# A fourth pair of split-weight tiles in place of one load buffer, and the fold products spread over four pieces

## The chip, the core and the metric

The kernel runs on one core of a Trainium2 chip. The metric is the device time of one execution in microseconds. A TensorE matmul is called PE here, its weight load PEld, VectorE is DVE, ScalarE is ACT, and SP is the queue that issues the loads.

## The reference, cut to what matters

Two layers of a decoder run over 256 tokens of width 1024. The change touches only the last part of the second layer, a mixture of eight experts:

```python
def moe_swiglu(t, router, w_gate, w_up, w_down):
    logits = (t @ router).astype(jnp.float32)
    top_logits, top_idx = lax.top_k(logits, TOP_K)          # TOP_K = 2 of 8
    gates = jax.nn.softmax(top_logits, axis=-1)
    combine = ...                                           # (tokens, experts)
    for e in range(N_EXPERTS):
        out = out + combine[:, e:e + 1] * swiglu(t, w_gate[e], w_up[e], w_down[e])

def swiglu(t, w_gate, w_up, w_down):
    return (jax.nn.silu(t @ w_gate) * (t @ w_up)) @ w_down  # 1024 -> 3584 -> 1024
```

All weights and activations are float32. The products keep nearly float32 precision: each float32 operand is split into a high part (a cast to fp32r) and a low part (what the cast left), and high by high, low by high and high by low are summed.

## The kernel before, in words

The experts are worked on one after the other, in the order of how many tokens they got, and alternate between two kinds (`KIND = "LSLSLSLS"`). A large one has room for 128 tokens. A small one has room for 64; the high and low parts of its 64 tokens lie side by side as the 128 columns of one stationary operand.

An expert's weights come in *pieces* of 128x1024 floats (512 KB), 84 for an expert. One load brings a unit of two pieces. `load` (L1182) takes its buffer from `ring`, a list of pools that is used round and round. At this stage the list holds 17 units: three of pool `wraw` (two 512 KB transfers each), two of `a8p`, one of `wraw3` (`NRAW3`), four of `wraw0` and seven of `wraw2`. SP issues a load as soon as its buffer is free, and a buffer is free when DVE has read its second piece.

`split_raw` (L181) makes a piece's pair of tiles out of pool `whl`, which holds three pairs: `split_to` (L188) lets ACT cast the piece to `whi` (L189), then DVE subtracts to get `wlo` (L190). A pair may be written again when PE has read it: the high tile after PE's products with it (L1497), the low tile after the products with the low part (L1499).

The order of the instructions on PE, ACT and DVE is that of the program (`in_order`); no engine overtakes within its own list. `piece` (L1488) first calls `run_ahead` (L1479), which writes down splits until `1 + AHEAD` pieces are split and not yet used, and then hands out the oldest. So with `AHEAD = 2` the split of piece n+2 stands in the lists before PE's products of piece n, and all that follows piece n in the program stands behind that split on ACT and DVE.

A group of twelve pieces is `gate_up` of one block of 512 hidden columns (L1501, four pieces for the gate, four for up; they are called g1 to g8 below) and `down` of the block before (L1568, four pieces, d1 to d4). A large expert's piece takes six products of 512 columns, a small one's four.

Small steps are laid between the pieces. `after(n, f)` (L1364) runs f behind the n-th piece from then on, as counted by `tick`. For a small expert `fold` (L1532) turns the two sums of a block and adds their halves:

- `turned` (L1538): eight products of 64 columns with the constant `fold` into one PSUM tile `hT`, all after the fourth piece (PE shows each float32 product as two instructions);
- `silu` on ACT (L1546) and `times` on DVE (L1551) after the eighth, `parts` after the eleventh, which splits the result into `mhh` (ACT, then DVE). `mhh` is the stationary operand of the next `down`.

The sums that `turned` reads are copied out of PSUM by ACT three pieces after their products (L1521). At the very end of the last expert the counts are 2, 3, 3 and 4.

`dispatch` (L1384) gathers the tokens of the next expert: DVE writes `sel` (L1392, L1394), PE multiplies with it (L1400, L1425), and ACT and DVE split the result into `X`. It is run in steps between the pieces of `down` of the fifth and sixth block. `combine` (L1583) adds an expert's result into `h` in the same way.

Of the kernel before, what the change touches and what calls it, by code (L numbers as in the profile page):

```python
# [11 lines left out]
F32R = mybir.dt.float32r  # L12
# [18 lines left out]
NEG = -1.0e30  # L31
NWRAW = 6
NRAW2 = 7
NRAW3 = 1
NRAW0 = 4
AHEAD = 2
PRE = 2


# [67 lines left out]
def build(tc, I, out, dbg=None, upto=99):  # L107
    with ExitStack() as es:
        _build(tc, tc.nc, es, I, out, dbg or {}, upto)


def _build(tc, nc, es, I, out, dbg, upto):
    const = es.enter_context(tc.tile_pool(name="const", bufs=1))
    wraw = es.enter_context(tc.tile_pool(name="wraw", bufs=NWRAW))
    whl = es.enter_context(tc.tile_pool(name="whl", bufs=3))
    small = es.enter_context(tc.tile_pool(name="small", bufs=2))

    def left(stack, name, bufs):
        return stack.enter_context(tc.tile_pool(name=name, bufs=bufs, reuse_waits="tile"))

    def right(stack, name, bufs):
        return stack.enter_context(tc.tile_pool(name=name, bufs=bufs, side="right", reuse_waits="tile"))
# [18 lines left out]
    def ps(shape, name, tag="ps"):  # L141
        return banks[tag].tile(shape, F32, name=name, tag=tag)
# [15 lines left out]
    def dump(name, ap):  # L158
        if name in dbg:
            nc.sync.dma_start(dbg[name], ap)  # L160
# [13 lines left out]
    def stream(src, n, piece=1024):  # L174
        raws = load_pieces(src, n, piece)

        def split(i):
            return split_raw(raws[i])
        return split

    def split_raw(raw):  # L181
        w = raw.shape[-1]
        hi = whl.tile([128, 1024], F32R, name="whi", tag="whi")
        lo = whl.tile([128, 1024], F32R, name="wlo", tag="wlo")
        split_to(hi[:, :w], lo[:, :w], raw)
        return hi[:, :w], lo[:, :w]

    def split_to(hi, lo, src):  # L188
        nc.scalar.copy(out=hi, in_=src)  # L189
        nc.vector.tensor_tensor(out=lo, in0=src, in1=hi.bitcast(F32), op=OP.subtract)  # L190
# [25 lines left out]
    def C(k):  # L216
        for offs, t in ((_COFF, cst), (_LOFF, csl), (_KOFF, csk)):
            if k in offs:
                o, n = offs[k]
                return t[:, o:o + n]  # L220
# [9 lines left out]
    def preload(func, after=None):  # L230

        after = eps if after is None else after.bitcast(F32)
        nc.scalar.activation(dummy, after, func, bias=eps, scale=0.0)
# [330 lines left out]
    with ExitStack() as l0:  # L564
# [272 lines left out]
        def finish(p, table=False):  # L837

            if not ya:
                ya.append(Blocks(4, "ya", b4))  # L840
            Yc = c4(Y[p])
            st = rt.tile([128, 3, 4], F32, name="st")
            nc.vector.tensor_scalar(st[:, 0, :], mv[p][:, :, 1], 64e-5, None, op0=OP.add)
            if table:
                nc.scalar.activation(st[:, 2, :], st[:, 0, :], AF.Sqrt)
            nc.vector.tensor_tensor(out=Yc, in0=Yc, in1=mv[p][:, :, 0:1].to_broadcast([128, 4, 64]), op=OP.subtract)
            if table:
                nc.vector.reciprocal(st[:, 2, :], st[:, 2, :])
            else:
                rsqrt(st[:, 2, :], st[:, 0, :], st[:, 1, :])  # L850
            bd = blockdiag("KR")[:, 0]
            for s in halves:
                nc.vector.tensor_tensor(out=bd[s, :, s], in0=Yc[s],
                                        in1=st[s, 2, :, None].to_broadcast([64, 4, 64]), op=OP.mult)
            yield
            g = ps([128, 4, 128], "yT", f"pp{p % 2}" if table else "ps")
            for c in range(4):
                nc.tensor.transpose(g[:, c, :], bd[:, c, :], ident)
            y_ = b1("yl")
            for s in halves:  # L860
                nc.vector.scalar_tensor_tensor(c4(y_[s]), g[s, :, s], V("lg", p)[s], c4(bonus[p][s]),
                                               op0=OP.mult, op1=OP.add)
            yield
            nc.vector.tensor_tensor(out=y_, in0=y_, in1=gg[p], op=OP.mult)
            hi, lo = ya[0](p)
            split_to(hi, lo, y_)
            yield
# [135 lines left out]
        end = [finish(2, True), finish(3, True)]  # L1003
# [21 lines left out]
    with ExitStack() as l0:  # L1025
# [40 lines left out]
        a8p = right(es, "a8", 2)  # L1066
# [23 lines left out]
    with l1:  # L1090
# [89 lines left out]
        ring = [wraw0] * NRAW0  # L1180

        def load(src, eng=None):  # L1182
            p = ring.pop(0)
            ring.append(p)
            if p is wraw:
                return stream(src, 2048)
            raw = a8([128, 2048], "mraw") if p is a8p else p.tile([128, 2048], F32, name="mraw", tag="mraw")
            (eng or nc.sync).dma_start(raw, src)
            return lambda i: split_raw(raw[:, i * 1024:(i + 1) * 1024])
# [167 lines left out]
    def experts(kinds, late=None, hook=None):  # L1357
# [6 lines left out]
        def after(n, f):  # L1364
            deferred.append([n, f])
# [112 lines left out]

        def run_ahead(n=1 + AHEAD):  # L1479
            while len(ready) < n and (raws or units):  # L1480
                if not raws:
                    load_unit()
                    if not units:
                        gf[0] = gain("final_norm", t=wraw.tile([128, D], F32, name="raw", tag="raw"), eng=nc.sync)
                sp, i = raws.pop(0)
                ready.append(sp(i))
# [14 lines left out]
        def gate_up(e, fc):  # L1501
            large = kinds[e] == "L"
            acc = []
            sums = {}
            for w in range(2):
                a = ps([128, 512], "gu", "gu")
                for i in range(4):
                    wh, wl = piece()
                    terms = []
                    for k in range(2):  # L1510
                        kb = 2 * i + k
                        c = slice(k * 512, (k + 1) * 512)
                        x = (X[e][:, 0, kb, :], X[e][:, 1, kb, :]) if large else X[e][:, kb, :]
                        terms.append((a, x, (wh[:, c], wl[:, c]), kb == 0, kb == 7))
                    products(large, terms)
                    tick()
                    next(side[0], None)
                acc.append(a)
                if not large:
                    t = sums[w] = mt.tile([128, 512], F32, name=("msg", "mhl")[w], **({} if w else {"bufs": 1}))  # L1520
                    after(1 if (e, fc) == (last, NFC - 1) else 3, lambda t=t, a=a: nc.scalar.copy(out=t, in_=a))  # L1521
            end = (e, fc) == (last, NFC - 1)
            if not large:
                return fold(sums, end)
            sgt = mt.tile([128, 512], F32, name="msg", bufs=1)
            nc.scalar.activation(sgt, acc[0], AF.Silu)
            if end:
                preload(AF.Sqrt)
            nc.vector.tensor_tensor(out=sgt, in0=sgt, in1=acc[1], op=OP.mult)
            return sgt  # L1530

        def fold(sums, end):  # L1532

            H = mt.tile([128, 4, 128], F32R, name="mhh")
            t = mt.tile([128, 512], F32, name="mhl").rearrange("p (w f t) -> p w f t", w=2, f=4)
            pt = []

            def turned():  # L1538
                pt.append(ps([128, 2, 4, 64], "hT", "hT"))
                for w in range(2):  # L1540
                    for f in range(4):
                        nc.tensor.matmul(pt[0][:, w, f, :], lhsT=sums[w][:, f * 128:(f + 1) * 128], rhs=C("fold"),
                                         start=True, stop=True)

            def silu():
                nc.scalar.activation(t[:, 0], pt[0][:, 0], AF.Silu)  # L1546
                if end:
                    preload(AF.Sqrt)

            def times():  # L1550
                nc.vector.tensor_tensor(out=t[:, 1], in0=t[:, 0], in1=pt[0][:, 1], op=OP.mult)  # L1551

            def parts():
                split_to(H[:, :, 0:64], H[:, :, 64:128], t[:, 1])
            for n, f in zip((2, 3, 3, 4) if end else (4, 8, 8, 11), (turned, silu, times, parts)):
                after(n, f)
            return H

# [126 lines left out]
    before.close()  # L1685
    mt = left(es, "moet", 2)
    mo = left(es, "moe", 1)
    wraw3 = left(es, "wraw3", NRAW3)
    ring[:0] = [wraw] * (NWRAW // 2) + [a8p] + [wraw3] * NRAW3
    dump("h3", h)  # L1690
    if upto <= 3:
        return
# [108 lines left out]
```

## Time and profile before

| | before |
|---|---|
| runs, median (lowest to highest) | 1545.63 us (1540.59 to 1546.87), 3 runs |
| the profiled execution, its time and its span | 1547.02 us, 1545.2 us |
| PE busy in the span | 1457.0 us (94%) |
| DVE busy | 1248.5 us (81%) |
| ACT busy | 1047.4 us (68%) |
| loads | 426.86 MB in all, mean 276 GB/s |

The page's table of slices shows that the experts fill the span from about 550 us to 1530 us. In that part PE and DVE have nine tenths or more in nearly every slice, and so do the DMA engines. Shares of busy time therefore don't tell what limits this part; it has to be read from single stretches. In the order of time a row gives the start, the length from the first start to the last end, and in brackets the idle time before it and what ended it. Instructions of one engine overlap at their ends, so the pace is read from one start to the next and not from the length. What a queue waits for is a row "who <- whom".

### The profile page before, as it was taken

Reading aid. Unit: us, or ns where it says so; the run is one execution under the profiler, and the core shown is the slowest. Engines: PE = TensorE matmul, PEld = TensorE weight load, DVE = VectorE, ACT = ScalarE, POOL = GpSimd, SP = SyncE. Lnnn points to the kernel's source line nnn. Section 1 sums busy time; section 2 is a strip of 40 time slices with the busy share of each in tenths; the row PEclk is TensorE's granted clock in tenths of the full one; section 3 lists DMA queues with packets and bytes.
Section 4 is the critical chain, followed back from the end, with each engine's and each line's share of the span. In section 5 each row is a group of like instructions: output and inputs, shape, how many; then the busy total and the mean of one; then the engine's idle time right before and its main releaser. Section 6 shows DMA issues by size and latency. Waiting matters only on the chain. (4 is left out here: it accounts for less than half of the span.)

```text
span 1545.2 us, 22471 instructions
## 1 busy us (share of the span) xinstructions
PE 1457.0 (94%) x7781; PEld 1196.7 (77%) x7781; DVE 1248.5 (81%) x1634; ACT 1047.4 (68%) x1440; POOL 85.6 (6%) x154
## 2 busy tenths in 40 slices
PE   7889999999999999999999999999999999999894
PEld 6879888998798887776778886678886667887673
DVE  6786775554586579989989989989989989989995
ACT  6634345444455568778878778878768878768884
POOL 4223120001010010000000000000000000000000
PEclk9999999999999999999999999999999999999997
DMA  8230035558453869989999989999989989999941
GB/s 303 67 108 15 1 97 190 186 183 298 152 191 116 320 235 351 345 329 375 395 364 374 369 329 378 384 371 377 361 337 372 383 360 382 372 352 349 368 181 32
DMA packets 78275, 426.86 MB, mean 276 GB/s; under 512 B 9200, under 2 KB 9472, under 8 KB 42560
## 3 DMA queue, kind: packets, MB, share of 16 engines
q1 hardware_dynamic: 77328, 422.38, 73.3%
q0 software_dynamic: 816, 2.87, 0.6%
q8 instruction: 65, 1.06, 0.3%
q14 instruction: 66, 0.54, 0.1%
HBM read 424.15 MB, written 1.05 MB: 275 GB/s over the span
## 5 line engine op out<-in xcount | busy, mean ns | idle before, releaser
L190 DVE TENSOR_TENSOR wlo<-mraw,whi 128x1024 fp32r<-128x1024 f32 x556 | 659.9, 1223 | 67.5 <-ACT whi L189 51.7
L189 ACT CAST whi<-mraw 128x1024 fp32r<-128x1024 f32 x556 | 570.6, 1050 | 151.3 <-PE gu L1497 79.6
L1497 PE MATMUL gu<-whi,x 128*128 128x512 f32 x1344 | 384.5, 394 | 0.6 <-ACT whi L189 0.5
L190 DVE TENSOR_TENSOR wlo<-raw,whi 128x1024 fp32r<-128x1024 f32 x232 | 280.3, 1222 | 109.2 <-ACT whi L189 104.9
L189 ACT CAST whi<-raw 128x1024 fp32r<-128x1024 f32 x232 | 239.6, 1043 | 135.6 <-PE acc L194 37.9
L1499 PE MATMUL gu<-wlo,x 128*128 128x512 f32 x896 | 291.6, 407 | 10.8 <-DVE wlo L190 10.3
L1497 PEld LDWEIGHTS gu<-whi,x 128*128 128x128 f32 x1344 | 250.2, 188 | 55.4 <-ACT whi L189 1.0
L1499 PEld LDWEIGHTS gu<-wlo,x 128*128 128x128 f32 x896 | 159.1, 188 | 82.4 <-DVE wlo L190 54.6
L1497 PE MATMUL Y<-whi,mhh 128*128 128x512 f32 x448 | 165.7, 411 | 19.9 <-DVE mhh L190 19.9
L1499 PE MATMUL Y<-wlo,mhh 128*128 128x512 f32 x448 | 144.9, 405 | 3.1 <-DVE wlo L190 2.2
L1497 PEld LDWEIGHTS Y<-whi,mhh 128*128 128x128 f32 x448 | 82.1, 190 | 45.4 <-DVE mhh L190 30.8
L1499 PEld LDWEIGHTS Y<-wlo,mhh 128*128 128x128 f32 x448 | 81.6, 190 | 34.2 <-DVE wlo L190 17.6
L193 PE MATMUL cp<-u,whi 128*128 128x256 f32 (+1 forms) x360 | 101.9, 283 | 0.0
L195 PE MATMUL cp<-u,whi 128*128 128x256 f32 (+1 forms) x360 | 101.8, 283 | 0.0
L194 PE MATMUL cp<-u,wlo 128*128 128x256 f32 (+1 forms) x360 | 101.8, 283 | 0.0
L1497 PE MATMUL Y<-whi,mhl 128*128 128x512 f32 x224 | 87.7, 391 | 0.0
L194 PEld LDWEIGHTS cp<-u,wlo 128*128 128x128 f32 (+1 forms) x360 | 68.3, 190 | 0.3
L193 PEld LDWEIGHTS cp<-u,whi 128*128 128x128 f32 (+1 forms) x360 | 68.3, 190 | 0.3
L195 PEld LDWEIGHTS cp<-u,whi 128*128 128x128 f32 (+1 forms) x360 | 68.3, 190 | 0.2
L1497 PEld LDWEIGHTS Y<-whi,mhl 128*128 128x128 f32 x224 | 42.2, 188 | 8.0
L193 PE MATMUL tp<-whi,u 128*128 128x512 f32 x96 | 40.6, 423 | 2.4 <-DVE u L190 2.4
L194 PE MATMUL tp<-whi,u 128*128 128x512 f32 x96 | 39.6, 413 | 2.2 <-DVE u L190 2.2
(425 smaller groups left out, 1967.5 us busy)
## 6 DMA issues: line engine op xcount, KB each, us to landing
mraw<-in_moe SPq DMA_DIRECT2D x277, 1024.0 KB, 7.0
raw<-in_moe SPq DMA_DIRECT2D x116, 512.0 KB, 6.6
raw<-in_ffn_gu SPq DMA_DIRECT2D x44, 512.0 KB, 3.7
raw<-in_w_in SPq DMA_DIRECT2D x38, 512.0 KB, 3.6
raw<-in_ffn_d SPq DMA_DIRECT2D x22, 512.0 KB, 3.5
raw<-in_w_out SPq DMA_DIRECT2D x16, 512.0 KB, 3.6
raw<-in_w_in SPq DMA_DIRECT2D x4, 416.0 KB, 9.0
h<-in_x SPq DMA_DIRECT2D x2, 512.0 KB, 6.1
```

Of the source, the lines that this page charges most:

```text
L189: nc.scalar.copy(out=hi, in_=src)
L190: nc.vector.tensor_tensor(out=lo, in0=src, in1=hi.bitcast(F32), op=OP.subtract)
L193: nc.tensor.matmul(o, lhsT=a[0], rhs=b[0], start=start, stop=False)
L194: nc.tensor.matmul(o, lhsT=a[1], rhs=b[0], start=False, stop=False)
L195: nc.tensor.matmul(o, lhsT=a[0], rhs=b[1], start=False, stop=stop)
L1497: nc.tensor.matmul(o, lhsT=x, rhs=b[0], start=start and i == 0, stop=False)
L1499: nc.tensor.matmul(o, lhsT=a[0] if large else a, rhs=b[1], start=False, stop=stop)
```

## The change

One load buffer is given up (`NRAW3` and pool `wraw3`, one unit of 1 MB), and its room goes to a new pool `whl2` with one pair of split tiles. `split_raw` takes its tiles from the four pairs in turn, and `AHEAD` becomes 3: the split of piece n+3 stands before PE's products of piece n. Before the experts begin there are three pairs as before.

The eight fold products are cut into four parts of two, placed after the second, third, fourth and fifth piece; `silu` goes from the eighth to the seventh, `times` stays at the eighth, and `parts` goes from the eleventh to the tenth. At the end of the last expert the counts stay.

```diff
--- before.py
+++ after.py
@@ -31,9 +31,8 @@
 NEG = -1.0e30
 NWRAW = 6
 NRAW2 = 7
-NRAW3 = 1
 NRAW0 = 4
-AHEAD = 2
+AHEAD = 3
 PRE = 2
 
 
@@ -178,10 +177,14 @@
             return split_raw(raws[i])
         return split
 
+    parts_ = [whl] * 3
+
     def split_raw(raw):
         w = raw.shape[-1]
-        hi = whl.tile([128, 1024], F32R, name="whi", tag="whi")
-        lo = whl.tile([128, 1024], F32R, name="wlo", tag="wlo")
+        p = parts_.pop(0)
+        parts_.append(p)
+        hi = p.tile([128, 1024], F32R, name="whi", tag="whi")
+        lo = p.tile([128, 1024], F32R, name="wlo", tag="wlo")
         split_to(hi[:, :w], lo[:, :w], raw)
         return hi[:, :w], lo[:, :w]
 
@@ -1535,12 +1538,12 @@
             t = mt.tile([128, 512], F32, name="mhl").rearrange("p (w f t) -> p w f t", w=2, f=4)
             pt = []
 
-            def turned():
-                pt.append(ps([128, 2, 4, 64], "hT", "hT"))
-                for w in range(2):
-                    for f in range(4):
-                        nc.tensor.matmul(pt[0][:, w, f, :], lhsT=sums[w][:, f * 128:(f + 1) * 128], rhs=C("fold"),
-                                         start=True, stop=True)
+            def turned(w, fs):
+                if not pt:
+                    pt.append(ps([128, 2, 4, 64], "hT", "hT"))
+                for f in fs:
+                    nc.tensor.matmul(pt[0][:, w, f, :], lhsT=sums[w][:, f * 128:(f + 1) * 128], rhs=C("fold"),
+                                     start=True, stop=True)
 
             def silu():
                 nc.scalar.activation(t[:, 0], pt[0][:, 0], AF.Silu)
@@ -1552,7 +1555,9 @@
 
             def parts():
                 split_to(H[:, :, 0:64], H[:, :, 64:128], t[:, 1])
-            for n, f in zip((2, 3, 3, 4) if end else (4, 8, 8, 11), (turned, silu, times, parts)):
+            for i in range(4):
+                after(2 if end else 2 + i, lambda i=i: turned(i // 2, range(2 * (i % 2), 2 * (i % 2) + 2)))
+            for n, f in zip((3, 3, 4) if end else (7, 8, 10), (silu, times, parts)):
                 after(n, f)
             return H
 
@@ -1685,8 +1690,8 @@
     before.close()
     mt = left(es, "moet", 2)
     mo = left(es, "moe", 1)
-    wraw3 = left(es, "wraw3", NRAW3)
-    ring[:0] = [wraw] * (NWRAW // 2) + [a8p] + [wraw3] * NRAW3
+    ring[:0] = [wraw] * (NWRAW // 2) + [a8p]
+    parts_.append(left(es, "whl2", 1))
     dump("h3", h)
     if upto <= 3:
         return
```

## Rows read from the trace of the kernel before

**Rows 1.** Busy time by stretch: a large expert, then a small one's DVE-paced stretch
```profile
core 0: us, PE busy (x) PEld busy (x) DVE busy (x) ACT busy (x) POOL busy (x), PEclk, DMA share, GB/s
805.00:925.00 120.00, 118.77 (x549) 97.63 (x548) 109.65 (x106) 93.12 (x102) 0.00 (x0) 1.00 0.95 358
925.00:1015.00 90.00, 84.20 (x373) 60.78 (x371) 85.44 (x85) 76.41 (x93) 0.00 (x0) 1.00 0.99 385
```

**Rows 2.** Waits in 925 to 1015 us: us in total, times, longest
```profile
DVE wlo L190 <- ACT whi L189: 4.5, 5, 1.5
PE Y L1497 <- DVE mhh L190: 2.8, 4, 1.1
```

**Rows 3.** The same view, 1406 to 1511 us, the last expert
```profile
DVE wlo L190 <- ACT whi L189: 5.3, 6, 1.5
```

**Rows 4.** DVE in order of time: start, length, what, count, idle before it
```profile
985.14 3.49 DVE L190 TENSOR_TENSOR wlo<-mraw,whi 128x1024 fp32r<-128x1024 f32 x3
988.55 3.49 DVE L190 TENSOR_TENSOR wlo<-raw,whi 128x1024 fp32r<-128x1024 f32 x3
992.79 2.36 DVE L190 TENSOR_TENSOR wlo<-raw,whi 128x1024 fp32r<-128x1024 f32 x2 [0.76 <-ACT whi L189]
```

**Rows 5.** ACT in order of time, same stretch
```profile
991.72 2.95 ACT L189 CAST whi<-raw 128x1024 fp32r<-128x1024 f32 x3 [1.29 <-PE gu L1497]
```

**Rows 6.** PE in order of time, same stretch
```profile
988.17 0.62 PE L1497 MATMUL Y<-whi,mhh 128*128 128x512 f32 x2
989.26 1.00 PE L1542 MATMUL hT<-csk,msg 128*128 128x64 f32 x8
990.10 1.06 PE L1542 MATMUL hT<-csk,mhl 128*128 128x64 f32 x8
990.96 0.71 PE L1497 MATMUL gu<-whi,x 128*128 128x512 f32 x2
991.52 0.63 PE L1499 MATMUL gu<-wlo,x 128*128 128x512 f32 x2
991.98 0.62 PE L1497 MATMUL gu<-whi,x 128*128 128x512 f32 x2
```

**Rows 7.** PE in order of time, a large expert
```profile
872.72 1.08 PE L1497 MATMUL gu<-whi,x 128*128 128x512 f32 x4
874.10 1.08 PE L1497 MATMUL gu<-whi,x 128*128 128x512 f32 x4
```

**Rows 8.** DVE in order of time, after a large expert
```profile
943.56 3.50 DVE L190 TENSOR_TENSOR wlo<-raw,whi 128x1024 fp32r<-128x1024 f32 x3 [1.48 <-ACT whi L189]
```

**Rows 9.** DVE and PE in order of time, dispatch of a large expert
```profile
1017.68 0.48 DVE L1392 TENSOR_SCALAR sel<-iota,route 128x128 f32<-128x128 int16 x2
1020.75 1.23 DVE L190 TENSOR_TENSOR wlo<-mraw,whi 128x1024 fp32r<-128x1024 f32 x1 [1.46 <-ACT whi L189]
...
1018.01 1.16 PE L1400 MATMUL xT<-sel,un 128*128 128x128 f32 x8 [1.28 <-DVE sel L1392]
```

**Rows 10.** Busy time by stretch: twelve pieces at two dispatches, two us within one
```profile
1008.97:1029.28 20.31, 18.03 (x100) 14.13 (x99) 15.05 (x17) 13.79 (x18) 0.00 (x0) 1.00 0.95 383
1248.85:1270.74 21.89, 19.59 (x100) 15.50 (x99) 15.05 (x17) 13.79 (x18) 0.00 (x0) 0.92 0.87 354
...
1258.00:1260.00 2.00, 2.00 (x10) 1.90 (x11) 1.17 (x2) 0.00 (x0) 0.00 (x0) 0.57 1.04 430
```

**Rows 11.** Waits in 805 to 925 us, a large expert
```profile
PE xT L1425 <- DVE sel L1394: 1.1, 1, 1.1
```

**Rows 12.** PE in order of time, first expert
```profile
627.73 0.73 PE L1499 MATMUL Y<-wlo,mhh 128*128 128x512 f32 x2 [0.78 <-DVE wlo L190]
```

**Rows 13.** SP's waits; DMA issues (count, size, us to landing); a late stretch
```profile
SPq L1188 <- DVE wlo L190: 513.7, 223, 6.4
...
mraw<-in_moe SPq DMA_DIRECT2D x241, 1024.0 KB, 7.1
...
1490.00:1500.00 10.00, 9.00 (x35) 5.97 (x35) 10.00 (x11) 9.25 (x13) 0.00 (x0) 1.00 0.00 0
```

## Prediction

> **What bounds the kernel now.** First the table of busy time, read for one large and one small expert apart. In the large one's 120 us PE is busy for 118.8 and DVE for 109.7: PE sets the pace, and DVE has idle time [rows 1]. In the 90 us behind it, most of a small expert, PE is busy for 84.2 by the profile's lengths, but DVE for 85.4, and here DVE is the later of the two [rows 1]. The view in order of time shows why. On DVE three splits follow the last three after 3.41 us, so a split costs 1.14 us [rows 4]. A large expert's piece costs PE 874.10 - 872.72 = 1.38 us, more than that [rows 7]; a small one's costs twice the 0.46 us from one pair of products to the next, 0.92 us, less than that [rows 6]. So the stage alternates: PE-paced for a large expert, DVE-paced for a small one, and a gain must come out of DVE's idle time in the small ones.
>
> That idle time is 4.5 us in 925 to 1015 us, all of it waiting for ACT's cast [rows 2]; two other small experts show the same 4.5, and the last, which has no dispatch behind it, 5.3 [rows 3]. A typical piece of it is the 0.76 us before 992.79 [rows 4]. ACT was not slow then: it had waited 1.29 us itself, for PE's products with the high part [rows 5]. PE in turn was in the block of fold products, which runs from 989.26 to 990.96, 1.70 us [rows 6]. It reads no split tile, so no pair comes free meanwhile.
>
> **The fourth pair in a small expert.** The cast for DVE's piece at 992.79 waited for the third piece before it, g1, whose high products ran from 990.96 to 991.52 [rows 6]; from there to DVE's start it took 1.27 us. DVE could have started at 992.79 - 0.76 = 992.03 [rows 4]. With four pairs the same cast waits for the piece one earlier, d4, whose high products ended by 988.8, before the fold [rows 6]. So it is early. The next DVE piece, due at 992.03 + 1.14 = 993.17, now waits for g1: 991.52 + 1.27 = 992.79, early by 0.4 us, even with the fold in one block. The cut of the fold helps further, since PE then never runs for longer than about 0.43 us (a quarter of 1.70) without freeing a tile. I take the whole 4.5 us as gone in three small experts and 5.3 us in the last: 18.8 us. PE has room for that: it waits 2.8 us for `mhh` alone in that stretch [rows 2], and each of its small pieces is 0.22 us shorter than DVE's.
>
> **One more piece in hand after a large expert.** In a large expert DVE waits for PE, so it can always be as far ahead as there are pairs; with four it enters the small expert one split further on. That is 1.14 us of the DVE-paced stretch done beforehand, at four such changes 4.5 us. It comes on top of the idle time: the 1.48 us at 943.56 is part of the 4.5 above [rows 8]. In the first expert small routing steps hold DVE up, and PE at last waits 0.78 us [rows 12]; I take 0.8 us for the piece in hand.
>
> **The later place behind the splits.** With `AHEAD` 3 everything after a piece stands behind one more split on ACT and DVE: the copies of the sums, `silu`, `sel`, the parts of `X` and `mhh`. `silu` and `parts` are moved one piece forward, so they stand behind the same split as before; the second copy is read one piece later, by the third fold pair, but the split before it hangs on PE's second piece and so is early; `times` has two pieces until `parts`. `X` is read at the soonest one piece behind its last part, and DVE's split before it is released by the same PE products as now; should it come late after all, that is 0 to 1.14 us a dispatch, which the dispatch rival below holds. What is left is `sel`. In a large expert PE waits 1.1 us for it [rows 11]. There DVE's last split before it is released by the same PE products as now (one split further, one pair more), so the wait stays. Before a large expert, in the DVE-paced stretch, PE waits 1.28 us until `sel` of 1017.68 is done [rows 9]. There it will wait one split longer, about 2.4 us, three times. DVE has done one more split by then, which it would otherwise have done after its idle 1.46 us [rows 9], so the two cancel in DVE's progress, and I take 0; the bounds are 0 and 1.14 us at each, 3.4 us.
>
> The longer wait has a second price. One of the three dispatches already shows it: the same twelve pieces took 21.89 us where those of another dispatch took 20.31, with a granted clock of 0.57 of full speed, close to the lower of its two levels (1.2 of 2.4 GHz), in the two us after PE had waited 1.28 us there [rows 9, 10]. That is 1.58 us for a fall. With PE idle for 2.4 us I take a fall at each of the three, two more than now: 3.2 us (bounds: -1.6, if the one goes too, and 3.2).
>
> **The cut of the fold, on PE.** The first piece behind the fold block starts its successor after 1.02 us, not 0.92, so leaving the block costs 0.1 us [rows 6]. Three more such breaks make 0.3 us for each fold. Where DVE sets the pace, that is hidden by PE's shorter pieces. It counts for the last two folds of a small expert, which lie in PE-paced work at the dispatch and the next large expert: six, 1.8 us. Bounds: 0, and 0.8 us a fold if a break cost more than twice as much.
>
> **The load buffer.** A unit is two pieces, 2.8 us of work. A load is issued when its buffer comes free, SP waits on DVE for 513.7 us in all for this and lands 1 MB 7.1 us after issue [rows 13]. With 17 units of about 2.8 us a unit is free 48 us before it is read again, so it lands some 41 us early, an estimate from these rows; with 16 units, 38. The end shows it directly: in 1490 to 1500 us nothing is transferred while DVE works without a gap [rows 13]. Cost 0; cover is 38 us, and without it each transfer would cost its 7.1 us.
>
> **The sum.** Gain 18.8 + 4.5 + 0.8 = 24.1 us; cost 3.2 + 1.8 = 5.0 us; net 19.1 us. The profiled execution (1547.02 us with its span of 1545.2) would come to 1527.9. It lies 1.4 us over the median of the runs, 1545.63; against that I forecast 1545.6 - 19.1 = 1526.5 us.
>
> **Rivals.**
>
> *The dispatch takes half of it back.* `sel` costs its 1.14 us at all seven dispatches (8.0 us) beside the falls of the clock and the breaks (5.0 us): 24.1 - 13.0 = 11.1 us of gain, 1534.5 us. For it: PE already waits at every dispatch [rows 9, 11]. Against it: the split before `sel` hangs on the same PE products in a large expert.
>
> *The loads are the bound.* Then nothing changes: 1545 us. For it: the DMA engines' share is 0.95 to 0.99 in these stretches [rows 1]. Against it: 385 GB/s in the small expert's stretch beside 358 in the large one's, so the rate follows the demand [rows 1], and SP waits for buffers. A gain of 24 us would also be covered by 38 us of data in hand. The Trainium skill ("DMA: Bandwidth & Descriptors", section "Where 436 GB/s comes from") puts the limit of loads from HBM at about 358 GB/s per core. By that rule the stage would already run at its limit and this change would bring nothing; the measured 385 GB/s over 90 us speaks against it [rows 1].
>
> *The pair brings no lead.* ACT stands in its own queue behind copies and `silu`, which now come one split later; were the lead eaten by that, only the breaks would be left: 1545.6 + 1.8 = 1547.4 us. Against it: ACT is busy for 76 of 90 us there and had idle time right before the late cast [rows 1, 5].
>
> *PE's clock falls in the small experts (slower).* Place: the fold pairs and the waits for `mhh` between them. Price: 1.58 us for a fall [rows 10]. It outweighs the rest of the sum (24.1 - 1.8 = 22.3 us) from 15 falls on; with one in each of the 28 folds it costs 44.2 us: 1567.5 us. Against it: with waits of up to 1.1 us for `mhh` the granted clock is 1.00 in the whole stretch [rows 1, 2], and the change makes PE's waits there shorter. The Trainium skill ("TensorE: Matmul & The Clock Gate", section "A second HAM failure mode: psum-queue depth-cycling") reports a kernel in which frequent short idle times made the clock swing; nothing of that shows in these rows.
>
> **How the numbers follow.** Forecast 0.62, more than that (under 1520) 0.03, dispatch 0.16, loads 0.06, no lead 0.07, clock 0.06. The range: at its lower end all of the gain with no break that counts and no fall of the clock, the one of now gone too, 1545.6 - 24.1 - 1.6 = 1520; at its upper the dispatch rival with the dearer breaks (six times 0.5 us more), 1534.5 + 3.0, rounded to 1538. That holds the forecast, the dispatch and the rest to 0.8. A measurement of this kernel tells 0.5%, 7.7 us, from no change: faster is under 1537.9, with 0.62 + 0.03 + 0.16 = 0.81; same 0.06 + 0.07 = 0.13; slower 0.06.
>
> **What would show it.** In the changed profile DVE's waits for the cast in a small expert should fall from 4.5 to under 1 us, its splits run on past the fold, and each of its groups of twelve pieces shorten by 0.7 to 0.8 us. The large experts should take as long as before. PE's wait for `sel` before a large expert should read about 2.4 us, with a granted clock under 1 behind it. SP should still wait for DVE. I would be wrong if DVE still waits for the cast by 0.5 us a group (the pair gives no lead), if ACT waits for loads, or if the large experts grow.

## The result, and the profile after

The changed kernel takes 1522.62 us (1520.67 to 1523.9, 4 runs) where the kernel before takes 1545.51 (4 runs): 22.9 us less, a ratio of 0.9856 with a 95% interval of 0.9831 to 0.9882. The forecast was 19.1 us less. The interval stands for 18.2 to 26.1 us, so the times alone don't tell the forecast from the measured median; the traces do.

The profiled execution took 1520.67 us with a span of 1518.7, 26.5 us under the span before. Of that, 2.4 us arose before 107 us in code that the change doesn't touch, and 2.0 us from the start of the last expert's last block on, so 22.1 us is what the experts give up to there. Of the 2.0 us, 1.57 come from the clock, and nothing seen here ties them to the change: PE waits 2.71 us before that block in both kernels, but only in the trace before does the granted clock fall behind the wait (0.50 of full speed in 1522 to 1524 us, 1.00 in 1496.5 to 1499 us after). PE in order of time, before and after:

```profile
1520.47 0.73 PE L1497 MATMUL Y<-whi,mhh 128*128 128x512 f32 x2 [2.71 <-DVE mhh L190]
...
1521.83 1.05 PE L1497 MATMUL Y<-whi,mhh 128*128 128x512 f32 x2
...
1495.90 0.73 PE L1500 MATMUL Y<-whi,mhh 128*128 128x512 f32 x2 [2.71 <-DVE mhh L193]
...
1496.93 0.63 PE L1500 MATMUL Y<-whi,mhh 128*128 128x512 f32 x2
```

The page's busy times in the span:

```profile
PE 1435.2 (95%) x7781; PEld 1203.5 (79%) x7781; DVE 1243.8 (82%) x1634; ACT 1047.1 (69%) x1440; POOL 86.0 (6%) x154
```

The counts of these engines are those of before and the shares rise by two points at most, so the stretches have to be read again.

The view of waits, 916 to 1002 us: the same small expert as in [rows 2], from its first group to the dispatch ("who <- whom", us in total, times, longest):

```profile
PE Y L1500 <- DVE mhh L193: 3.8, 5, 0.9
ACT whi L192 <- PE gu L1500: 3.3, 10, 0.3
...
DVE wlo L193 <- ACT whi L192: 0.2, 1, 0.2
```

DVE waits 0.2 us for the cast where it waited 4.5. In the last expert the same row reads 0.2 as well, up to its last two blocks, where it read 5.3 [rows 3].

Busy time by stretch: a large expert, the small one behind it, the dispatch (columns as in [rows 1]):

```profile
797.00:916.00 119.00, 117.87 (x543) 96.75 (x542) 108.95 (x106) 91.76 (x100) 0.00 (x0) 1.00 0.96 364
916.00:1002.00 86.00, 81.16 (x381) 63.44 (x379) 85.70 (x87) 77.55 (x95) 0.00 (x0) 1.00 1.00 400
1002.00:1024.00 22.00, 19.03 (x99) 16.04 (x100) 15.44 (x17) 13.84 (x19) 0.00 (x0) 0.92 0.90 352
```

In the second row DVE is busy for 85.70 of 86 us: the small expert now runs as fast as DVE can. The large one is PE-paced as before, though its groups got a little longer (last section). DVE in order of time, around a fold of the third small block; it answers to [rows 4]:

```profile
973.21 11.43 DVE L193 TENSOR_TENSOR wlo<-mraw,whi 128x1024 fp32r<-128x1024 f32 x10
984.56 0.41 DVE L1554 TENSOR_TENSOR mhl<-mhl,hT 128x256 f32<-128x256 f32 x1
984.89 2.35 DVE L193 TENSOR_TENSOR wlo<-mraw,whi 128x1024 fp32r<-128x1024 f32 x2
987.16 0.42 DVE L193 TENSOR_TENSOR mhh<-mhl,mhh 128x256 fp32r<-128x256 f32 x1
987.49 3.49 DVE L193 TENSOR_TENSOR wlo<-mraw,whi 128x1024 fp32r<-128x1024 f32 x3
```

No row has idle time before it. From 973.21 to 987.49 us, 14.28 us, lies one group: twelve splits of 1.137 us and two small steps of 0.33 us make 14.30. Before, a group took 15.14 us. PE in order of time, the fold cut in four; it answers to [rows 6]:

```profile
973.34 0.74 PE L1500 MATMUL Y<-whi,mhh 128*128 128x512 f32 x2 [0.73 <-DVE mhh L193]
...
975.32 0.55 PE L1545 MATMUL hT<-csk,msg 128*128 128x64 f32 x4
975.68 0.71 PE L1500 MATMUL Y<-whi,mhh 128*128 128x512 f32 x2
976.23 0.62 PE L1502 MATMUL Y<-wlo,mhh 128*128 128x512 f32 x2
976.68 0.55 PE L1545 MATMUL hT<-csk,msg 128*128 128x64 f32 x4
```

A part of the fold takes 0.36 us, and the piece behind it starts its low products 0.55 us after the high ones instead of 0.46. Last, the dispatch of a large expert, PE and then DVE; it answers to [rows 9]:

```profile
1001.92 0.74 PE L1500 MATMUL Y<-whi,mhh 128*128 128x512 f32 x2 [0.74 <-DVE mhh L193]
1002.50 0.63 PE L1502 MATMUL Y<-wlo,mhh 128*128 128x512 f32 x2
1005.52 1.16 PE L1403 MATMUL xT<-sel,un 128*128 128x128 f32 x8 [2.40 <-DVE sel L1395]
1006.44 1.10 PE L1500 MATMUL Y<-whi,mhh 128*128 128x512 f32 x2
...
1002.91 2.36 DVE L193 TENSOR_TENSOR wlo<-mraw,whi 128x1024 fp32r<-128x1024 f32 x2
1005.18 0.48 DVE L1395 TENSOR_SCALAR sel<-iota,route 128x128 f32<-128x128 int16 x2
1005.58 1.22 DVE L193 TENSOR_TENSOR wlo<-mraw,whi 128x1024 fp32r<-128x1024 f32 x1
...
1013.01 1.23 DVE L193 TENSOR_TENSOR wlo<-mraw,whi 128x1024 fp32r<-128x1024 f32 x1 [3.13 <-ACT whi L192]
```

PE waits 2.40 us for `sel`, and two high products right behind take 1.10 us instead of 0.62 to 0.71. This stands at all three dispatches of a large expert. DVE has idle time of its own a few us later (3.13 us). The granted clock behind PE's wait is 0.51 of full speed, close to the lower of its two levels (1.2 of 2.4 GHz), as busy time by stretch shows:

```profile
1006.50:1010.00 3.50, 3.50 (x15) 3.11 (x14) 1.52 (x2) 1.53 (x2) 0.00 (x0) 0.51 1.04 413
```

**Where the time came from.** The same PE product is looked up in both traces, and its start after the change is subtracted from its start before; what this difference gains from one place to the next is what a stretch gave ("by the PE starts" below). From the first expert's first product to the last block of the last expert:

| stretch | forecast, us | measured, us |
|---|---|---|
| first expert | 0.8 | 1.2 |
| three small experts, up to the dispatch | 3 x (4.5 + 1.14) = 16.9 | 3 x 5.76 = 17.3 |
| last small expert | 5.3 + 1.14 = 6.4 | 6.6 |
| dispatches of large experts | -2 x 1.58 = -3.2 | -1.49, -1.46, +0.11 |
| from behind a dispatch to the next small expert, three together | -1.8 | -0.15 |
| sum | 19.1 | 22.1 |

### The profile page after: what moved, and what is told of

It reads as the page before. It is cut to its first block, busy times and chain, and to the rows that moved or that the text cites. A ratio compares the mean times of both kernels' runs of the same rounds, so it can differ in the third digit from the quotient of the medians.

```text
span 1518.7 us, 22486 instructions
## 1 busy us (share of the span) xinstructions
PE 1435.2 (95%) x7781; PEld 1203.5 (79%) x7781; DVE 1243.8 (82%) x1634; ACT 1047.1 (69%) x1440; POOL 86.0 (6%) x154
## 5 line engine op out<-in xcount | busy, mean ns | idle before, releaser
L193 DVE TENSOR_TENSOR wlo<-mraw,whi 128x1024 fp32r<-128x1024 f32 x546 | 645.3, 1221 | 49.4 <-ACT whi L192 43.0
L192 ACT CAST whi<-mraw 128x1024 fp32r<-128x1024 f32 x546 | 559.9, 1050 | 118.5 <-PE Y L1500 54.8
L193 DVE TENSOR_TENSOR wlo<-raw,whi 128x1024 fp32r<-128x1024 f32 x242 | 291.3, 1221 | 107.7 <-ACT whi L192 100.6
L192 ACT CAST whi<-raw 128x1024 fp32r<-128x1024 f32 x242 | 250.1, 1043 | 132.6 <-PE acc L197 37.9
L1502 PE MATMUL gu<-wlo,x 128*128 128x512 f32 x896 | 282.6, 397 | 3.6 <-DVE wlo L193 2.4
L1502 PEld LDWEIGHTS gu<-wlo,x 128*128 128x128 f32 x896 | 165.0, 188 | 53.1 <-DVE wlo L193 17.8
L1500 PE MATMUL Y<-whi,mhh 128*128 128x512 f32 x448 | 171.3, 422 | 20.9 <-DVE mhh L193 20.5
L1502 PE MATMUL Y<-wlo,mhh 128*128 128x512 f32 x448 | 141.5, 397 | 0.5
```

The source lines that it names most:

```text
L1500: nc.tensor.matmul(o, lhsT=x, rhs=b[0], start=start and i == 0, stop=False)
L1502: nc.tensor.matmul(o, lhsT=a[0] if large else a, rhs=b[1], start=False, stop=stop)
```

## The experiments

The theory: DVE's pace is what bounds a small expert, its idle time came from the high tile that came free too late, and the fourth pair removes it; the place behind one more split makes `sel` late and lets the clock fall; the loads have time in hand. The rivals: the cut of the fold does it; the loads bound; the late `sel` costs nothing beyond the clock.

**The pair without the cut.** The fold stays in one block behind the fourth piece.

```diff
-                after(2 if end else 2 + i, lambda i=i: turned(i // 2, range(2 * (i % 2), 2 * (i % 2) + 2)))
+                after(2 if end else 4, lambda i=i: turned(i // 2, range(2 * (i % 2), 2 * (i % 2) + 2)))
```

> The changed kernel with the eight fold products in one block behind the fourth piece, as before; the fourth pair, AHEAD 3 and the places of silu, times and parts stay. Theory (the pair alone removes DVE's stall, since the cast then waits for the piece ahead of the fold): same as the changed kernel within 2 us, 1521 to 1525 us, and DVE's waits for the cast in the DVE-paced stretch of a small expert stay under 1 us. Rival (the cut of the fold does half of it): DVE waits 0.3 to 0.4 us in each of the 26 groups of the small experts, 8 to 10 us more, 1531 to 1533 us.

Measured: 1526.46 us beside 1548.01 before, a ratio of 0.9858 (0.9844 to 0.9873), within 0.0002 of the changed kernel's. The time itself is 1.5 us over the range that was expected, but the kernel before took 2.5 us more in this comparison too. DVE's waits for the cast in 920 to 1006 us:

```profile
DVE wlo L193 <- ACT whi L192: 0.6, 1, 0.6
```

A group of twelve pieces by busy time:

```profile
971.00:985.29 14.29, 13.55 (x66) 10.54 (x65) 14.29 (x16) 13.12 (x17) 0.00 (x0) 1.00 1.02 417
```

PE in order of time, the fold:

```profile
981.40 1.00 PE L1545 MATMUL hT<-csk,msg 128*128 128x64 f32 x8
982.24 1.06 PE L1545 MATMUL hT<-csk,mhl 128*128 128x64 f32 x8
983.11 0.71 PE L1500 MATMUL gu<-whi,x 128*128 128x512 f32 x2
983.66 0.62 PE L1502 MATMUL gu<-wlo,x 128*128 128x512 f32 x2
```

DVE is busy for all of a group's 14.29 us with the fold in one block, so the pair, with its place in the lists, carries nearly all of the change. The block takes 983.11 - 981.40 = 1.71 us and 0.09 us behind it, 1.80; four parts take 4 x (0.36 + 0.09) = 1.80. The cut costs nothing. By the PE starts the experts of this kernel gain 21.0 us, 1.1 less than with the cut.

**The cut without the pair.** To the kernel before, with three pairs and `AHEAD` 2, only this is done:

```diff
-            for n, f in zip((2, 3, 3, 4) if end else (4, 8, 8, 11), (turned, silu, times, parts)):
+            for i in range(4):
+                after(2 if end else 2 + i, lambda i=i: turned(i // 2, range(2 * (i % 2), 2 * (i % 2) + 2)))
+            for n, f in zip((3, 3, 4) if end else (8, 8, 11), (silu, times, parts)):
```

> The kernel before with its fold products cut into four pairs behind the second to fifth piece; three pairs of tiles, AHEAD 2, 17 units, and silu, times and parts at 8, 8 and 11. Theory (the pair does the work): PE still runs late by the waits for mhh and by four cuts of 0.37 us, the cast for the piece three on comes about 0.5 us late instead of 0.76; 4 to 8 us less than before, 1538 to 1542 us. Rival (the cut does the work): 1523 to 1529 us.

Measured: 1537.34 us beside 1548.01, a ratio of 0.9935 (0.9922 to 0.9947). The gain of 10.7 us is over the 4 to 8 expected, a miss, and far from the rival's. DVE's waits in 918 to 1010 us:

```profile
DVE wlo L190 <- ACT whi L189: 1.3, 4, 0.6
```

A row of DVE in order of time there, behind a fold:

```profile
989.83 2.36 DVE L190 TENSOR_TENSOR wlo<-raw,whi 128x1024 fp32r<-128x1024 f32 x2 [0.16 <-ACT whi L189]
```

The wait at a fold fell from 0.76 us [rows 4] to 0.16, and groups take 14.76 us. So cut and pair remove the same idle time by two ways: alone they give 10.7 and 21.6 us, together 22.9 in another comparison. By the PE starts a small expert gains 2.5 us with the cut alone and 5.6 with the pair alone. What the pair has beyond the cut is the rest of the wait and the piece in hand.

**One load buffer less.** The kernel before without `wraw3`, 16 units.

```diff
-    ring[:0] = [wraw] * (NWRAW // 2) + [a8p] + [wraw3] * NRAW3
+    ring[:0] = [wraw] * (NWRAW // 2) + [a8p]
```

> The kernel before without the load buffer of pool wraw3: 16 units instead of 17, nothing else. Theory: loads land some 38 us before they are read instead of 41, no change, 1543 to 1548 us. Rival (the store of loads counts): slower by at least 3 us, the 2.8 us of one unit or more.

Measured: 1547.27 us beside 1548.01, a ratio of 0.9995 (0.9986 to 1.0004): no change.

**Nine units instead of 17**, the kernel before with its 17-unit list cut behind the ninth:

```diff
+    del ring[9:]
```

> The kernel before with nine units of load buffers in use instead of 17. Theory (nothing waits for loads): they land about 9 x 2.8 - 7 = 18 us before they are read, no change within 3 us of the kernel before. Rival (the loads are near the bound, the store evens out the stretches): slower by 5 us or more, ACT waits for transfers.

Measured: 1548.24 us beside 1546.53, a ratio of 1.0010 (1.0001 to 1.0020). The stretch of [rows 1]:

```profile
925.00:1015.00 90.00, 84.36 (x375) 61.01 (x373) 85.41 (x86) 76.39 (x94) 0.00 (x0) 1.00 0.99 388
```

DVE is as busy as with 17 units, and the transfers take the same share of the DMA engines. The shortest time from a load's landing to the first cast of it was 9.6 us, and by the PE starts the experts take as long as before, to 0.01 us. So eight buffers, 8 MB, can be given up for 1.7 us (3.1 at the interval's upper end), and in the profiled execution none of that lies in the experts.

**Four pairs, but `AHEAD` 2**, in the changed kernel, with the old counts of `silu` and `parts`:

```diff
-AHEAD = 3
+AHEAD = 2
-            for n, f in zip((3, 3, 4) if end else (7, 8, 10), (silu, times, parts)):
+            for n, f in zip((3, 3, 4) if end else (8, 8, 11), (silu, times, parts)):
```

> The changed kernel with AHEAD 2: four pairs of tiles, but sel, copies and parts stand behind one split less; silu and parts back at 8 and 11. Theory (the lead comes from the number of pairs, and sel's later place costs PE 1.1 us and a fall of its clock at each of three dispatches): PE waits about 1.28 us for sel instead of 2.40, falls of the clock at none to one of three, the small experts' groups still 14.3 us; 1518 to 1522 us. Rival (the place in the lists gives the lead, the pair alone doesn't): DVE waits for the cast again, 0.5 to 0.76 us a group, 1533 to 1542 us.

Measured: 1518.85 us beside 1548.01, a ratio of 0.9818 (0.9806 to 0.9831): 29.2 us less, better than the change: by the PE starts its experts gain 28.0 us, not 22.1. PE at the dispatch:

```profile
1006.12 1.16 PE L1403 MATMUL xT<-sel,un 128*128 128x128 f32 x8 [1.26 <-DVE sel L1395]
1007.03 0.70 PE L1500 MATMUL Y<-whi,mhh 128*128 128x512 f32 x2
```

The wait is back near the 1.28 us of [rows 9], and the clock falls at none of the three. Before a small expert PE waits 0.80 us, less than the 1.1 of [rows 11], which was not expected. The order in the lists, not the number of tiles, makes `sel` late. What this version loses is more than half of the piece in hand: at a change from a large to a small expert about 0.5 us is left of 1.15.

**`sel` early.** In the changed kernel the step that makes `sel` stands before the pieces of the sixth block's `gate_up`, not behind them; the gathers keep their place (`behind`, not shown, puts an empty step where the first one stood).

```diff
+                if fc == NFC - 3 and e < last:
+                    nxt = dispatch(e + 1)
+                    next(nxt)
                 if fc + 1 < NFC:
                     nx = gate_up(e, fc + 1)
...
-                    nxt = dispatch(e + 1)
+                    nxt = behind(nxt)
                     side[0] = until_parts(nxt)
```

> The changed kernel with the two sel instructions of a dispatch written twelve pieces' worth earlier, before the gate_up that precedes it; the gathers stay where they are. Theory (the later place of sel costs 1.12 us at four dispatches of a small expert and, through the fall of the clock behind the 2.40 us wait, some 1.4 us at three of a large one, and the rest of that wait is DVE's own pace): no falls of the clock at the dispatches, waits for sel gone, 7 to 12 us less than the changed kernel, about 32 us less than the kernel before. Rival (the falls come from the gathers or the waits for mhh, not from sel): the three falls stay, 4 us less at most.

Measured: 1506.18 us beside 1546.53, a ratio of 0.9741 (0.9728 to 0.9754): 40.4 us less than before, 17.5 more than the change gave in its own comparison (17.1 by the PE starts). DVE, then PE in order of time around the dispatch:

```profile
990.13 0.47 DVE L1395 TENSOR_SCALAR sel<-iota,route 128x128 f32<-128x128 int16 x2
...
998.71 0.62 PE L1502 MATMUL Y<-wlo,mhh 128*128 128x512 f32 x2
999.16 1.05 PE L1403 MATMUL xT<-sel,un 128*128 128x128 f32 x8
```

The stretch of the dispatch by busy time:

```profile
998.00:1020.00 22.00, 21.29 (x121) 18.27 (x122) 19.25 (x19) 18.12 (x24) 0.00 (x0) 1.00 1.02 407
```

`sel` is done 8.6 us before PE needs it; PE's gather follows without idle time, at the full clock. The expectation was a miss: 7 to 12 us, because I held that DVE, which paces a small expert, would take part of PE's wait back elsewhere. It didn't. The waits in the changed kernel were 3 x 2.40 + 4 x 1.12 = 11.7 us, with three falls of the clock 16.4, nearly the whole 17.5. The rows suggest why: with the gathers PE has more to do for a while, and DVE stands idle a few us behind `sel` (1.46 us in [rows 9], 3.13 us in the row of the changed kernel at 1013.01), so DVE isn't the pace there and PE's lost time is not made good.

**Idle products in place of the wait.** In the changed kernel eight products of 512 columns in bf16 stand before the first gather of a large expert; nothing uses their result.

```diff
+                        if q == 0:
+                            t = ps([128, 512], "warm")
+                            for _ in range(8):
+                                nc.tensor.matmul(t, lhsT=onesb, rhs=onesb[:, None, :].to_broadcast([128, 4, 128]),
+                                                 start=True, stop=True)
                         pts[q] = ps([128, 4, 128], "xT")
```

> The changed kernel with eight idle products (bf16, 512 columns, results unused) on PE before the first gather of a large expert's dispatch, in the 2.40 us in which PE waits for sel. It takes the fall of the clock apart from the wait. Theory: the wait itself stays (DVE writes sel when it did), the clock does not fall at the three dispatches; some 1.4 us each, 4 to 5 us less than the changed kernel, 27 us less than the kernel before. Rival (the falls come from other waits, or the idle products cost what they save): 22 to 24 us less than the kernel before.

Measured: 1519.91 us beside 1548.97, a ratio of 0.9818 (0.9803 to 0.9833): 29.1 us less than before, where 27 was expected; by the PE starts its experts gain 4.7 us more than those of the changed kernel. PE in order of time at the dispatch:

```profile
1004.49 0.62 PE L1507 MATMUL Y<-wlo,mhh 128*128 128x512 f32 x2
1004.95 1.90 PE L1454 MATMUL warm<-onesb 128*128 128x512 bf16 x8
1007.52 1.16 PE L1403 MATMUL xT<-sel,un 128*128 128x128 f32 x8 [0.67 <-DVE sel L1395]
1008.44 0.70 PE L1505 MATMUL Y<-whi,mhh 128*128 128x512 f32 x2
```

The stretch by busy time:

```profile
1004.00:1026.00 22.00, 20.75 (x114) 16.67 (x115) 17.05 (x18) 15.45 (x20) 0.00 (x0) 1.00 0.95 375
```

The gather starts as late as before, 3.0 us behind the last low products, but the clock stays at its full level. By the PE starts the second round of a small and a large expert gains 5.84 us here and 4.28 in the changed kernel: 1.56 us is the price of a fall alone (1.61 and 1.59 in the two other rounds), beside the forecast's 1.58. With `sel` early the round gains 9.51 us: 3.67 us more, about the two waits (2.40 and 1.12) by themselves.

**`sel` early with `AHEAD` 2**, both edits together.

> The same earlier sel on the kernel with four pairs and AHEAD 2. Theory: its waits for sel (0.80 us four times, 1.27 us three times) go, 5 to 7 us less than that kernel, 34 to 36 us less than the kernel before. Rival (with sel early the place in the lists is all that AHEAD changes, so AHEAD 3 with early sel is as good): within 2 us of the other kernel of this call with early sel.

Measured: 1510.73 us beside 1546.53, a ratio of 0.9771 (0.9758 to 0.9784): 35.8 us less, as expected, and 4.5 us longer than with `AHEAD` 3 in the same comparison. Once `sel` no longer hangs on it, the place one split further is worth these 4.5 us; by the PE starts 3.6 of them lie in the experts, 1.1 in the first one and 2.4 at the changes from a large to a small one behind it.

**Five pairs**, with `sel` early: `AHEAD` 4, `NRAW2` 6, the counts 6, 7 and 9.

> Five pairs of tiles, AHEAD 4, 15 units of loads, silu, times and parts at 6, 7 and 9, with the early sel. It measures the piece in hand: DVE's stall in a small expert is gone already with four pairs, so all that a fifth can bring is one split more done at each of four changes from a large to a small expert. Theory: 4 to 5 us less than four pairs with AHEAD 3 and early sel. Rival (the piece in hand is not worth a piece; what the first expert or the ends do is): within 1.5 us of it, or slower.

Measured: 1505.0 us, a ratio of 0.9733 (0.9720 to 0.9746), only 1.2 us under `sel` early with four pairs, where 4 to 5 were expected: a miss, and what the rival had said. By the PE starts the fifth pair does give 1.3 us at each of four changes from a large to a small expert. In the first expert, where DVE also does the last routing steps, it loses 2.4 us at one place and 1.2 on the whole, and 2.0 at the end: 0.47 by a longer wait before the last block (3.16 us) and 1.55 by a fall of the clock behind it, which the trace of four pairs happens to lack. The place in the first expert, PE in order of time:

```profile
627.30 0.65 PE L1567 MATMUL hT<-ident,msg 128*128 128x128 f32 x4 [2.21 <-DVE msg L1532]
627.71 0.60 PE L1500 MATMUL Y<-whi,mhh 128*128 128x512 f32 x1
```

A step that PE waits for stands behind one more split, and the clock falls (0.60 us for a product that takes 0.40).

**Five pairs, but four pieces ahead at both ends**, in the first expert and in the last two blocks of the last.

```diff
-        def run_ahead(n=1 + AHEAD):
+        def run_ahead(n=None):
+            n = n or depth[0]
...
+                depth[0] = AHEAD - (e == last and fc >= NFC - 2) + (e > 0)
```

> Five pairs and early sel as in the run before, but only four pieces are split ahead through the first expert and from the last expert's sixth group on; five in between. Theory (the fifth pair is worth 1.3 us at each change, which a 2.21 us wait of PE with a fall of the clock in the first expert and a longer wait at the end had eaten): that wait and its fall go, 2 to 4 us less than five pairs throughout, 42 to 45 us less than the kernel before. Rival (the fifth pair brings nothing over four): within 1.5 us of it.

Measured: 1504.19 us beside 1548.97, a ratio of 0.9709 (0.9695 to 0.9723): 44.8 us less, as expected, and the best of all; it is 3.3 us more than five pairs throughout gave, each beside its own kernel before. The row of the first expert that answers to the one above; no fall of the clock follows it:

```profile
627.25 0.66 PE L1569 MATMUL hT<-ident,msg 128*128 128x128 f32 x4 [0.56 <-DVE msg L1534]
```

## Why the prediction was right, point by point

- *DVE sets the pace of a small expert, and its 4.5 us can go.* Right. The wait fell from 4.5 to 0.2 us [rows 2], in the last expert from 5.3 to 0.2 [rows 3], and groups shortened by 15.14 - 14.29 = 0.85 us where 0.7 to 0.8 was forecast. That the pair does it even with the fold in one block is shown by the kernel without the cut; that the cut alone would also remove most of this wait (4.5 to 1.3 us), the forecast didn't say.
- *One more piece in hand, 1.14 us at a change.* Right: a small expert gave 5.76 us where 4.5 + 1.14 was forecast. It needs the place in the lists as well as the tiles: with `AHEAD` 2 about 0.5 us of it is left.
- *The first expert, 0.8 us.* It gave 1.2, but at another place than the one named, so the closeness is in part luck. PE reached `down` of the third block 1.7 us sooner, since pieces before it (614 to 622 us in the trace before) wait less for the split. The wait of 0.78 us [rows 12] gave nothing: one of 0.56 us for `msg` stands near that place, as in the row of the last experiment. The longer pieces of a large expert (last section) gave some 0.5 us back.
- *`sel` before a large expert, 2.4 us three times, and a fall at each.* Right: 2.40 us and a fall of the granted clock (0.51 in the row above) at three of three. The two dispatches that had no fall before cost 1.49 and 1.46 us, a fall of 1.56 to 1.61 and nothing besides, and the third, which had a fall before [rows 10], cost nothing. That it was two falls more hangs on the one trace of before: the trace with 16 units shows a fall at none of its three dispatches, the one with nine units at one. So the cancelling held: the wait grew by the idle time that DVE had had there anyway. What the sum didn't show is what all seven waits cost in absolute terms, 11.7 us, which were there to be had, as `sel` early shows.
- *`sel` before a small expert unchanged.* Right, 1.12 us [rows 11].
- *The breaks of the fold, 1.8 us.* Here a term was mis-sized. The 0.1 us behind the block was counted for three more breaks, but four parts of 0.36 us are also 0.26 us shorter than the block of 1.70: both ways come to 1.80 us. From behind the second dispatch to the next small expert's first piece the gain hardly moves (12.16 and 12.15 us), but there the longer pieces of the large expert (0.45 us, last section) and a gain of as much before them cancel, so the price is better told by the rows and by the kernel without the cut, beside which the cut even gives 1.1 us. This term (1.65 us), the first expert (0.4), the small experts (0.5 together) and the dispatches (0.3) make up the 3 us by which the forecast was short of the 22.1.
- *The load buffer, 0.* Right: no change with 16 units, and 1.7 us with nine. The estimates of 41 and 38 us between landing and reading were too long: it is 30.7 us at the shortest and 38.8 at the median before, 25.2 and 34.2 in the changed kernel, which is still cover enough. The view of waits puts 4.1 us of DVE's idle time in the changed kernel down to transfers (the longest 3.3 us, at the first dispatch of a large expert), but those loads had landed 25 us or more before, and the same idle time at the second dispatch, 3.13 us, is put down to ACT. The rival of the loads is out: the rate rose to 400 GB/s in the small expert's stretch. The Trainium skill ("DMA: Bandwidth & Descriptors", section "Where 436 GB/s comes from") has a limit of about 358 GB/s per core for loads from HBM, and these rows lie above it. The Trainium skill's "HBM Reference" (section "Specifications (TRN2)") puts a core that streams alone at about 425; the 400 GB/s agree with that.
- *The rival of the dispatch* had its mechanism (a longer wait, a fall) but charged the wait on top; the *rival of the clock* in the small experts doesn't show, the granted clock in 916 to 1002 us is 1.00. *No lead* is out by the 0.2 us.
- *The signs.* DVE's wait, the length of the groups, `sel` and the clock read as foretold. One sign that the prediction named against itself did show: the large experts grew, by some 0.45 us each. The gain of the small experts outweighs it, but the prediction had nothing for it.

## What to carry to other kernels

Before a buffer or a lead is added, find the step whose pace remains when every wait is gone (here DVE's 1.137 us a split) and sum the waits of that engine alone; with the piece in hand this forecast 23.4 us for the four small experts, which gave 23.9. A lead made by putting work earlier in an in-order list makes every small step behind it late; such a step that another engine waits for is moved forward by itself, which here was worth three quarters as much again (17.5 us beside 22.9). And a wait cost about its full length here (3.67 us for 2.40 and 1.12) where the engine that paces the stretch was idle too: look at both engines in that stretch before a wait is called hidden.

## What the runs showed of the hardware

- With four pairs, two of each four pieces in a large expert take 1.387 us instead of 1.373, in the change and with `AHEAD` 2 alike, with the fold in one block too; with three pairs all take 1.373 [rows 7]. PE in order of time in the changed kernel, each row the first products of a piece:

```profile
867.39 1.08 PE L1500 MATMUL gu<-whi,x 128*128 128x512 f32 x4
...
868.76 1.09 PE L1500 MATMUL gu<-whi,x 128*128 128x512 f32 x4
...
870.15 1.09 PE L1500 MATMUL gu<-whi,x 128*128 128x512 f32 x4
...
871.53 1.08 PE L1500 MATMUL gu<-whi,x 128*128 128x512 f32 x4
```

  That is 0.07 us for a group of twelve (16.94 to 17.01 us) and some 1.8 us in all four large experts. Why was not tested.
- The length of a wait of PE alone did not tell whether the granted clock fell. After 2.40 us it fell in three of three places in the changed kernel, and in three of three with the pair alone. After 1.26 to 1.28 us (with 0.74 us shortly before) it fell in one of three in the kernel before and with nine units, in none of three with 16 units, in two of three with the cut alone and in none with `AHEAD` 2. After the 2.70 to 2.72 us before the last block it fell in nine of eleven kernels; the changed kernel and the one with `sel` early kept the full clock there. Eight idle products kept it up at each dispatch, with 0.67 us of idle time left.
- A switch from the fold's 64-column products back to 512-column ones costs PE 0.09 us, behind a short part as behind the whole block, and the parts together are shorter by as much as the three more switches cost: cutting the block in four was free here (1.80 us either way).
